# A two-directional gated scan inside an encoder layer: the base of eight tokens replaced by three more halving levels

## The chip, the core and the metric

The kernel runs on one core of a Trainium2 chip. The core has five engines that run side by side and wait for each other through semaphores: PE (TensorE, matmuls; its weight loads are shown as PEld), DVE (VectorE, elementwise work), ACT (ScalarE, activations and copies), POOL (GpSimd) and SP (SyncE, which issues most transfers). The metric is the device time of one execution in microseconds; lower is better. A profile is one execution with every instruction's start and duration.

## What is computed

One encoder layer for 1024 tokens of width 1024. The normed input is projected into the columns of two token mixers: a convolution module, and a two-directional recurrence (HGRN2) of 8 heads with 128 channels. The recurrence is what the change touches:

```python
def _chunk_gated_scan(q, k, v, lf):
    """S_t = diag(f_t) S_{t-1} + k_t v_t^T,  o_t = S_t^T q_t"""
...
def _bi_hgrn2(q, v, z_fwd, z_bwd, lb_fwd, lb_bwd):
    lf_f, k_f = _forget_log_and_key(z_fwd, lb_fwd)
    lf_b, k_b = _forget_log_and_key(z_bwd, lb_bwd)
    o_fwd = _chunk_gated_scan(qh, heads(k_f), vh, heads(lf_f))
    flip = lambda t: jnp.flip(t, axis=1)
    o_bwd = flip(_chunk_gated_scan(flip(qh), flip(heads(k_b)), flip(vh), flip(heads(lf_b))))
    return o_fwd + o_bwd
```

The weight between a query at token t and a key at token s is a sum over channels of q, k and the product of all forget gates f between s and t. After the mixers come output projections, a gated feed-forward part and a last norm. The large projections make up most of the matmuls; each float32 product is made of three products of split operands (high x high, high x low, low x high: lines 147 to 149).

## The kernel before

**Stages.** First norm and first projections; the paired projections with the convolution beside them; the scan stage (about 490 to 905 us in the profile), in which the rest of the projections (`dense`) is threaded between the scan's own steps; output projections; the feed-forward part; the last projection.

**The order of work.** PE runs in the order in which the program is written. The other engines' order is chosen by a scheduler when the kernel is built, from what each instruction depends on. The scan's loop runs over 8 heads and 2 halves of 512 tokens each: 16 half heads. After each piece of scan work it calls `between`, which first issues `FILL` = 1.3 pieces of `dense` (a piece is 6 matmuls of 128x512), then `BASE_STEPS` steps of the next half head's base (`ahead`), then one step of the previous head's outputs (`pending`). A half head has seven such pieces: four levels, two transposes and one product for the states.

**The scan of one half head.** The weights between tokens are built by halving: at level h, blocks of 2h tokens are split in two, and one product gives the weights between the two halves of every block, for both directions at once, since a pair (s, t) belongs to the forward direction on one side of the diagonal and to the backward direction on the other. For that, qF holds each query times the product of the gates from its block's middle, kG each key likewise, and tb the product over each whole block. After a level, kG and qF of half of the tokens are multiplied by tb of the neighbouring block, and tb itself is doubled. All channels lie on the 128 partitions, tokens along the free dimension.

- `scan_inputs` (L1072): loads q and the gate inputs z, and makes the keys `kk` and the gates f (ACT), then clamps f on DVE (L1093).
- `scan_base` (L1096): makes, for blocks of 8 tokens, products of gates within the block from its middle in tile DE and their reciprocals (L1117), from these Qh and Kh (scaled so that Qh times Kh is right for any pair within 8 tokens), then qF, kG and tb for blocks of 8. All of it is on DVE. `tt` (L1061) is the helper that issues every DVE multiplication, `keys` (L1064) that of the keys.
- `scan_levels` (L1156): `inside` (L1193) multiplies Kh by Qh for each 32 tokens, in both directions, into a bank "sc"; `level` (L1181) does levels 8 and 16 with a copy `A_t` of the keys on ACT (L1179), level 8 into the same bank, level 16 into bank "ob"; `blocks` (L1207) does levels 32 and 64. Each level is followed by the multiplications of kG, qF and tb. Masked copies on DVE (L1245 to L1249) gather the weights of each 32 tokens in D_t; the diagonal goes by tile dg and an addition (L1250). ACT puts all into S_t (L1252, L1254).
- `scan_states` (L1257): transposes kG (L1264) and multiplies it with v (L1273); `scan_outputs` (L1296) makes the outputs in bank "ob" (L1314).

**Banks.** PSUM has eight banks: three "mm" for `dense`, two "sc", two "tr", one "ob". Taking a bank again waits until its last reader has finished.

Of the kernel before, what the change touches and what calls it, by code (L numbers as in the profile page):

```python
# [29 lines left out]
BASE_STEPS = 2  # L30
# [16 lines left out]
def tile_hybrid_encoder(  # L47
# [868 lines left out]
    m_f, m_b, m_d, m_16 = [cp.tile([P, 32], U8, name=n) for n in ("m_f", "m_b", "m_d", "m_16")]  # L916

    def build_masks():
        it = mp.tile([P, 32], I32, tag="tm", name=nm("it"), bufs=4)
        ip = mp.tile([P, 32], I32, tag="tm", name=nm("ip"), bufs=4)  # L920
        G.iota(it, pattern=[[1, 32]], base=0, channel_multiplier=0)
        for g in range(0, P, 32):
            G.iota(ip[g : g + 32, :], pattern=[[0, 32]], base=0, channel_multiplier=1)
        xo = mp.tile([P, 32], I32, tag="tm", name=nm("xo"), bufs=4)
        V.tensor_tensor(xo, it, ip, op=ALU.bitwise_xor)
        fs = mp.tile([P, 4, 32], F32, tag="tm", name=nm("fs"), bufs=4)
        V.tensor_copy(fs[:, 0, :], xo)
        V.tensor_tensor(fs[:, 1, :], it, ip, op=ALU.subtract)
        ge = fs[:, 1, :]
        V.tensor_scalar(m_d, fs[:, 0, :], 0.0, None, op0=ALU.is_equal)  # L930
        V.tensor_scalar(m_16, fs[:, 0, :], 16.0, None, op0=ALU.is_ge)
        V.tensor_scalar(fs[:, 2, :], fs[:, 0, :], 8.0, None, op0=ALU.is_lt)
        V.tensor_scalar(fs[:, 3, :], ge, 0.0, None, op0=ALU.is_ge)
        V.tensor_tensor(m_f, fs[:, 2, :], fs[:, 3, :], op=ALU.mult)
        V.tensor_scalar(fs[:, 3, :], ge, 0.0, None, op0=ALU.is_lt)
        V.tensor_tensor(m_b, fs[:, 2, :], fs[:, 3, :], op=ALU.mult)
# [111 lines left out]
    NB = H // 8  # L1048
    DE = hp.tile([P, 2, 2, H], F32, name="DE")
    dg = hp.tile([P, 4, 32], F32, name="dg")  # L1050
    none = hp.tile([P, H], mybir.dt.bfloat16, name="none")
    E0, D0 = 0, 2 * H
    for o in (E0 + 3, D0 + 3):
        G.memset(view(DE, o, [[8, 2 * NB]]), 1.0)
    G.memset(none, 0.0)
    G.memset(dg, 0.0)

    N2 = 2 * NB

    def tt(o, a, b, op=ALU.mult):  # L1060
        V.tensor_tensor(o, a, b, op=op)  # L1061

    def keys(o, a, scale, b):
        V.scalar_tensor_tensor(o, a, scale, b, op0=ALU.mult, op1=ALU.mult)  # L1064
# [7 lines left out]
    def scan_inputs(i):  # L1072
# [5 lines left out]
        kk = hp.tile([P, 2, H], F32, tag="k", name=nm("k"), bufs=2)  # L1078
        nc.sync.dma_start(q, d_q[h][half])
        for d in range(2):  # L1080
            z = page(hp, "zi", 3)
            nc.sync.dma_start(z, d_z[d][h][half])
            A.activation(kk[:, d, :], z, AF.Sigmoid, scale=-1.0)
            A.activation(z, z, AF.Sigmoid)
            fo = view(f, d * H + 7 * d, [[8, NB], [1 - 2 * d, 8]])
            A.activation(
                fo,
                z.rearrange("p (b e) -> p b e", e=8),
                AF.Identity,
                scale=oml_of(d, h),  # L1090
                bias=lb_of(d, h),
            )
        V.tensor_scalar(f, f, MIN_FORGET, 1.0, op0=ALU.max, op1=ALU.min)  # L1093
        return q, f, kk, kscale[:, h : h + NH + 1 : NH]

    def scan_base(ins):  # L1096


        q, f, kk, ks = ins

        def two(t, *r):
            if len(r) == 1:
                return view(t, r[0], [[8, N2]])
            return view(t, r[0], [[r[1] - r[0], 2], [8, N2]])

        fv = lambda *r: two(f, *r)
        ed = lambda *r: two(DE, *r)
        D = D0


        V.tensor_copy(ed(2, D + 4), fv(3, 4))
        tt(ed(1, D + 5), fv(2, 4), fv(3, 5))
        yield
        tt(ed(0, D + 6), fv(1, 6), ed(1, D + 5))
        tt(ed(D + 7), ed(D + 6), fv(7))
        yield
        V.reciprocal(ed(D, 7), ed(0, D + 7))  # L1117
        yield

        fm = hp.tile([P, 2, NB], F32, tag="fm", name=nm("fm"), bufs=2)  # L1120
        turned = view(fm, NB, [[-NB, 2], [1, NB]])
        tt(turned, view(f, 0, [[H, 2], [8, NB]]), view(DE, E0, [[H, 2], [8, NB]]))
        tb = hp.tile([P, 3, NB], F32, tag="tb", name=nm("tb"), bufs=3)
        tt(tb[:, 0:2, :], turned, view(DE, D + 7, [[H, 2], [8, NB]]))
        V.tensor_copy(tb[:, 2, :], tb[:, 0, :])
        tt(ed(D + 1, 6), ed(D, 7), fv(1, 7))
        yield
        tt(ed(D + 2, 5), ed(D + 1, 6), fv(2, 6))
        tt(ed(4), ed(5), fv(5))
        yield  # L1130

        qF = hp.tile([P, 2, H], F32, tag="qF", name=nm("qF"), bufs=3)
        kG = hp.tile([P, 2, H], F32, tag="kG", name=nm("kG"), bufs=2)
        Qh = hp.tile([P, 2, H], F32, tag="Qh", name=nm("Qh"), bufs=1)
        Kh = hp.tile([P, 2, H], F32, tag="Kh", name=nm("Kh"), bufs=1)
        along = [[8, NB], [1, 8]]
        for d in range(2):
            m0, st = ((0, 1), (7, -1))[d]
            whole = [[8, NB], [st, 8]]
            tt(view(Qh, (1 - d) * H + m0, whole), view(q, m0, whole), view(DE, D + d * H, along))  # L1140
            yield
            keys(
                view(Kh, d * H + m0, whole),
                view(kk, d * H + m0, whole),
                ks[:, d : d + 1],
                view(DE, d * H, along),
            )
            yield
        both = [[H, 2], [8, NB], [1, 8]]
        tt(view(qF, 0, both), view(Qh, 0, both), view(fm, 0, [[NB, 2], [1, NB], [0, 8]]))  # L1150
        yield
        tt(view(kG, 0, both), view(Kh, 0, both), view(DE, D + 7, [[H, 2], [8, NB], [0, 8]]))
        yield
        yield qF, kG, [(Qh[:, 1 - d, :], Kh[:, d, :]) for d in range(2)], tb

    def scan_levels(base, S_t, Tt):  # L1156


        qF, kG, qk, tb = base

        def pairs(t, h):
            return view(t, 0, [[2 * h, H // (2 * h)], [H + h, 2], [1, h]])


        def near(t):
            return t.rearrange("p (c t) -> p c t", c=4)

        def slot(b, n):
            return b[:, n * P : (n + 1) * P]

        def each():
            for c in range(4):
                for g in range(0, P, 32):
                    yield c * P + g, slice(g, g + 32), slice(32 * c, 32 * c + 32)

        def level(b, h):

            A_t = page(hp, "A", 2)
            A.copy(A_t.rearrange("p (b x e) -> p b x e", x=2, e=h), pairs(kG, h))  # L1179
            for at, g, o in each():  # L1180
                T.matmul(  # L1181
                    b[g, o].rearrange("p (b x e) -> p b x e", x=2, e=h),
                    A_t[:, at : at + 32],
                    view(qF, at, [[2 * h, 16 // h], [H + h, 2], [1, h]]),
                    start=True,
                    stop=True,
                )

        def inside(b):

            for d in range(2):
                for at, g, o in each():
                    T.matmul(  # L1193
                        slot(b, 1 + d)[g, o],
                        qk[d][1][:, at : at + 32],
                        qk[d][0][:, at : at + 32],
                        start=True,
                        stop=True,
                    )
# [15 lines left out]
        def over(m):  # L1215
            return view(m, 0, [[0, 4], [1, 32]])

        D_t = hp.tile([P, 4, 32], F32, tag="D", name=nm("D"), bufs=2)
        b = bank("sc")
        inside(b)  # L1220
        for h in (8, 16, 32, 64):
            n, nb = H // (2 * h), H // h
            if h < 32:
                if h == 16:
                    b = bank("ob")
                level(b, h)
# [5 lines left out]
            tt(pairs(kG, h), pairs(kG, h), view(tb, 1, [[2, n], [nb - 1, 2], [0, h]]))  # L1232
            tt(pairs(qF, h), pairs(qF, h), view(tb, nb + 1, [[2, n], [nb - 1, 2], [0, h]]))
            if h < 64:
                tn = hp.tile([P, 3, NB], F32, tag="tb", name=nm("tb"), bufs=3)
                k = 3
                to = view(tn, 0, [[n, 3], [1, n]])
            else:
                k = 2
                to = view(Tt, 0, [[4, 2], [1, n]])  # L1240
            tt(to, view(tb, 0, [[nb, k], [2, n]]), view(tb, 1, [[nb, k], [2, n]]))
            tb = tn
            if h == 8:
                A.copy(D_t, near(slot(b, 0)))
                V.copy_predicated(D_t, over(m_f), near(slot(b, 1)))  # L1245
                for o, m in ((D_t, m_b), (dg, m_d)):
                    V.copy_predicated(o, over(m), near(slot(b, 2)))
            elif h == 16:
                V.copy_predicated(D_t, over(m_16), near(slot(b, 0)))  # L1249
                V.tensor_tensor(D_t, D_t, dg, op=ALU.add)  # L1250
# [135 lines left out]
    dense.fill(21)  # L1386
    pending = Stream(iter(()))
    for h in range(NH):
# [4 lines left out]
        for half in range(2):  # L1393
# [21 lines left out]
            qF, kG = base[0], base[1]  # L1415
# [403 lines left out]
```

## Time and profile before

| | |
|---|---|
| median of 3 runs | 1782.89 us (1781.95 to 1783.09) |
| profiled execution | 1784.03 us, of which 1782.3 us from its first to its last instruction (the span) |
| PE / DVE / ACT busy in the span | 1730.3 / 1257.5 / 773.8 us |
| mean granted TensorE clock | 0.993 |

How to read the lines in the next parts. A line of the waits is: who (engine, tile, line) waited for whom, total us, how many times, the longest. A line of the time line is: start in us, duration, engine, line, operation, output <- inputs, shape, number of merged instructions, and in brackets idle time before it and what ended it. A line of a group is: line, engine, operation, output <- inputs, shape, count, then busy us and mean ns of one, then the engine's idle time before these instructions. A line of a stretch is: from:to, length, then busy us and count of each engine in the order of its header. Matmuls overlap: dense ones start 0.23 us apart though each is shown with 0.39 us. A float32 matmul leaves two records.

### The profile page before, as it was taken

What the parts mean: (1) busy time and instruction counts of PE and PEld (TensorE: products, weight loads), DVE (VectorE), ACT (ScalarE), POOL (GpSimd) and SP (SyncE); (2) the same over time, 40 slices, a digit from 0 to 9 for tenths busy, and PEclk for the clock granted to TensorE, in tenths of its full rate; (3) what the DMA queues carried; (4) which work ended last, traced back from release to release, by engine and by line L of the source; (5) the groups of instructions that cost most, each with busy time, mean ns of one, the idle gap of its engine ahead of it and who ended that gap; (6) DMA issues with size and microseconds to landing.
All of it is one profiled execution on the core that took longest, in us unless ns stands there. A gap on an engine that the chain in (4) does not pass through costs nothing.

```text
span 1782.3 us, 27603 instructions
## 1 busy us (share of the span) xinstructions
PE 1730.3 (97%) x10614; PEld 1415.1 (79%) x10614; DVE 1257.5 (71%) x1892; ACT 773.8 (43%) x1486; POOL 153.7 (9%) x168
## 2 busy tenths in 40 slices
PE   8999999999999999999999999999999999999997
PEld 6878787888877777778878888778888888888885
DVE  5599999747679999999545567667667667444455
ACT  7343433334455656565551344344344344422123
POOL 2201111000000000000000002011111111000000
PEclk9999999999999999999999999999999999999998
DMA  8657787746663333435367665567767666534233
GB/s 286 216 154 179 189 185 183 197 152 207 195 190 109 117 119 120 131 102 189 126 209 223 189 207 182 149 147 149 153 150 155 144 150 136 159 103 127 76 91 136
DMA packets 321258, 284.29 MB, mean 160 GB/s; under 512 B 14942, under 2 KB 242022, under 8 KB 321126
## 3 DMA queue, kind: packets, MB, share of 16 engines
q1 hardware_dynamic: 279958, 250.01, 44.4%
q0 software_dynamic: 41168, 32.51, 12.8%
q8 instruction: 83, 1.36, 0.3%
q14 instruction: 49, 0.40, 0.1%
HBM read 189.40 MB, written 76.81 MB: 149 GB/s over the span
## 4 chain that ended last, share of the span: by engine, by line
PE 65%; DVE 16%; DMA 7%; issue 6%; ACT 4%; POOL 1%; SPq 0%; POOLq 0%; DVEq 0%; ACTq 0%
PE mm L147 16%; PE mm L148 16%; PE mm L149 16%; PE sc L147 3%; PE sc L149 3%; PE sc L148 3%; DVE acc L956 3%; DMA sw<-in_w_in_dram 3%; DVE kG L1061 2%; DVE wp L123 2%; DVE qF L1061 2%; DVE DE L1061 1%; PE tr L149 1%; PE tr L147 1%; PE tr L148 1%
## 5 line engine op out<-in xcount | busy, mean ns | idle before, releaser
L147 PE MATMUL mm<-hx,wp 128*128 128x512 f32 x1144 | 462.5, 404 | 9.9 <-DVE ev L718 4.7
L149 PE MATMUL mm<-hx,wp 128*128 128x512 f32 x1144 | 449.5, 393 | 1.4 <-DVE wp L123 1.4
L148 PE MATMUL mm<-hx,wp 128*128 128x512 f32 x1144 | 448.9, 392 | 0.0
L123 ACT CAST wp<-wr 128x1024 fp32r<-128x1024 f32 (+2 forms) x171 | 162.1, 949 | 352.9 <-PE mm L148 227.4
L147 PEld LDWEIGHTS mm<-hx,wp 128*128 128x128 f32 x1144 | 216.6, 189 | 57.0 <-DVE ev L718 7.6
L149 PEld LDWEIGHTS mm<-hx,wp 128*128 128x128 f32 x1144 | 216.3, 189 | 49.5 <-DVE wp L123 2.5
L123 DVE TENSOR_TENSOR wp<-wr,wp 128x1024 fp32r<-128x1024 f32 (+2 forms) x169 | 185.8, 1100 | 92.0 <-ACT wp L123 80.1
L148 PEld LDWEIGHTS mm<-hx,wp 128*128 128x128 f32 x1144 | 216.7, 189 | 41.1 <-issue 0.2
L956 DVE SCALAR_TENSOR_TENSOR acc<-gl,v_b,acc 128x1024 f32<-128x1024 f32 x120 | 149.0, 1277 | 0.5
L1670 DVE TENSOR_TENSOR xr<-mm,xr 128x512 f32<-128x512 f32 x48 | 33.2, 691 | 72.9 <-PE mm L149 72.9
L367 ACT COPY su<-mm 128x512 f32<-128x512 f32 x82 | 47.4, 578 | 56.2 <-PE mm L149 55.2
L123 ACT CAST wq<-sw 128x1024 fp32r<-128x1024 f32 x41 | 43.1, 1050 | 63.8 <-PE mm L148 29.8
L1519 DVE SCALAR_TENSOR_TENSOR tm<-gp,v_a,tm 128x512 f32<-128x512 f32 x88 | 65.9, 749 | 2.0
L147 PE MATMUL mm<-hy,wp 128*128 128x512 f32 x164 | 64.7, 395 | 2.0 <-ACT su L367 2.0
L147 PE MATMUL sc<-hy,wq 128*128 128x512 f32 x164 | 64.6, 394 | 0.0
L148 PE MATMUL mm<-hy,wp 128*128 128x512 f32 x164 | 64.3, 392 | 0.0
L149 PE MATMUL sc<-hy,wq 128*128 128x512 f32 x164 | 64.2, 391 | 0.0
L147 PE MATMUL tr<-hx,wp 128*128 128x512 f32 x164 | 63.9, 390 | 0.0
L149 PE MATMUL tr<-hx,wp 128*128 128x512 f32 x164 | 63.8, 389 | 0.0
L148 PE MATMUL tr<-hx,wp 128*128 128x512 f32 x164 | 63.8, 389 | 0.0
L148 PE MATMUL sc<-hy,wq 128*128 128x512 f32 x164 | 63.8, 389 | 0.0
L149 PE MATMUL mm<-hy,wp 128*128 128x512 f32 x164 | 63.7, 389 | 0.0
(362 smaller groups left out, 3413.8 us busy)
## 6 DMA issues: line engine op xcount, KB each, us to landing
wr<-in_w_in_dram SPq DMA_DIRECT2D x56, 512.0 KB, 4.3
wr<-in_ffn_w_up_dram SPq DMA_DIRECT2D x24, 512.0 KB, 6.1
sw<-in_ffn_w_up_dram SPq DMA_DIRECT2D x44, 256.0 KB, 3.3
d_g<-ft SPq DMA_DIRECT2D x44, 256.0 KB, 3.3
sw<-in_ffn_w_up_dram POOLq DMA_DIRECT2D x20, 512.0 KB, 8.6
sw<-in_w_in_dram SPq DMA_DIRECT2D x38, 256.0 KB, 3.2
d_z<-ev SPq DMA_DIRECT2D x32, 256.0 KB, 3.8
zi<-d_z SPq DMA_DIRECT2D x32, 256.0 KB, 2.6
```

Of the source, the lines that this page charges most:

```text
L123: parts = A.copy(hi, src), eng.tensor_tensor(lo, src, hi.bitcast(F32), op=ALU.subtract)
L147: T.matmul(acc, whi[:, k, :], ahi, start=first, stop=False, skip_group_check=again)
L148: T.matmul(acc, whi[:, k, :], alo, start=False, stop=False, skip_group_check=again)
L149: T.matmul(acc, wlo[:, k, :], ahi, start=False, stop=last, skip_group_check=again)
L367: A.copy(t, acc)
L956: V.scalar_tensor_tensor(acc, g[:, k : k + S], tap(k), acc, op0=ALU.mult, op1=ALU.add)
L1061: V.tensor_tensor(o, a, b, op=op)
L1519: V.scalar_tensor_tensor(c, g[:, o + k : o + k + H], vec("fdw", k * NF + j), c, op0=ALU.mult, op1=ALU.add,)
L1670: V.tensor_tensor(xr[i][half], acc, xr[i][half], op=ALU.add)
```

## The change

The base for blocks of 8 tokens goes, with DE, its reciprocals, Qh, Kh, fm and dg. In its place the same halving starts at blocks of one token:

- kG is made from the keys by one scaling per direction; qF is q times the gates of the other direction; tb is f itself.
- `scan_base` of the next half head now has five steps: scaling, key copy and qF; the diagonal's products (q with kG of both directions, accumulated) and level 1; level 2; level 4; the copies into D_t. Its PE products go into the four quarters of one "sc" bank. So PE work, which the base didn't have, is now issued in `between`, ahead of `pending`.
- `BASE_STEPS` becomes 1. The first half head's base is issued step by step within the opening fill, which stays at 21 pieces.
- `scan_levels` starts at level 8, whose bank is now "ob", as level 16's was and is. The key copy for a level is issued right after the multiplication of kG before it.
- The views `pairs` run over one half of the tile and then the other, where they alternated before. tb has two parts in place of three.
- Tiles: qF has 4 buffers (3 before), kG 3 (2; it takes the place of `kk`), A_t 3 (2), D_t 3 (2).

```diff
-BASE_STEPS = 2
+BASE_STEPS = 1
...
         f = hp.tile([P, 2, H], F32, tag="f", name=nm("f"), bufs=2)
-        kk = hp.tile([P, 2, H], F32, tag="k", name=nm("k"), bufs=2)
+        kG = hp.tile([P, 2, H], F32, tag="kG", name=nm("kG"), bufs=3)
...
+    def pairs(t, h, other=H):
+
+        return view(t, 0, [[other + h, 2], [2 * h, H // (2 * h)], [1, h]])
+
+    def key_blocks(kG, h):
+        A_t = page(hp, "A", 3)
+        A.copy(pairs(A_t, h, 0), pairs(kG, h))
+        return A_t
...
+    def level(b, A_t, qF, h):
+
+        for at, g, o in each():
+            T.matmul(
+                b[g, o].rearrange("p (b x e) -> p b x e", x=2, e=h),
+                A_t[:, at : at + 32],
+                view(qF, at, [[2 * h, 16 // h], [H + h, 2], [1, h]]),
+                start=True,
+                stop=True,
             )
...
+    def double(kG, qF, tb, h, to=None):
+
+        n, nb = H // (2 * h), H // h
+        tt(pairs(kG, h), pairs(kG, h), view(tb, 1, [[nb - 1, 2], [2, n], [0, h]]))
+        tt(pairs(qF, h), pairs(qF, h), view(tb, nb + 1, [[-(nb + 1), 2], [2, n], [0, h]]))
+        if to is None:
+            tn = hp.tile([P, 2, n], F32, tag=f"tb{h}", name=nm("tb"), bufs=2)
+            to = view(tn, 0, [[n, 2], [1, n]])
+        else:
+            tn = None
+        tt(to, view(tb, 0, [[nb, 2], [2, n]]), view(tb, 1, [[nb, 2], [2, n]]))
+        return tn
 
     def scan_base(ins):
...
+        q, f, kG, ks = ins
+        qF = hp.tile([P, 2, H], F32, tag="qF", name=nm("qF"), bufs=4)
+        D_t = hp.tile([P, 4, 32], F32, tag="D", name=nm("D"), bufs=3)
+        for d in range(2):
+            V.tensor_scalar(kG[:, d, :], kG[:, d, :], ks[:, d : d + 1], None, op0=ALU.mult)
+        A_t = key_blocks(kG, 1)
+        tt(qF, view(q, 0, [[0, 2], [1, H]]), view(f, H, [[-H, 2], [1, H]]))
         yield
...
+        b = bank("sc")
+        for at, g, o in each():
+            for d in range(2):
+                T.matmul(
+                    slot(b, 3)[g, o],
+                    kG[:, d, at : at + 32],
+                    q[:, at : at + 32],
+                    start=d == 0,
+                    stop=d == 1,
+                )
+        tb = f
+        for n, h in enumerate((1, 2, 4)):
+            level(slot(b, n), A_t, qF, h)
+            tb = double(kG, qF, tb, h)
+            A_t = key_blocks(kG, 2 * h)
             yield
...
+        A.copy(D_t, near(slot(b, 2)))
+        for n, m in ((0, m_1), (1, m_2), (3, m_d)):
+            V.copy_predicated(D_t, over(m), near(slot(b, n)))
+        yield qF, kG, A_t, tb, D_t
...
         for h in (8, 16, 32, 64):
-            n, nb = H // (2 * h), H // h
             if h < 32:
-                if h == 16:
-                    b = bank("ob")
-                level(b, h)
+                b = bank("ob")
+                level(slot(b, 0), A_t, qF, h)
...
             if h == 8:
-                A.copy(D_t, near(slot(b, 0)))
-                V.copy_predicated(D_t, over(m_f), near(slot(b, 1)))
-                for o, m in ((D_t, m_b), (dg, m_d)):
-                    V.copy_predicated(o, over(m), near(slot(b, 2)))
+                A_t = key_blocks(kG, 16)
+                V.copy_predicated(D_t, over(m_8), near(slot(b, 0)))
             elif h == 16:
                 V.copy_predicated(D_t, over(m_16), near(slot(b, 0)))
-                V.tensor_tensor(D_t, D_t, dg, op=ALU.add)
...
-    dense.fill(21)
+    dense.fill(6)
+    for _ in range(5):
+        cur.step(1)
+        dense.fill(3)
```

Level 1, 2 and 4 and the diagonal are 16, 16, 16 and 32 matmuls of 128x32 per half head; `inside`, which goes, was 32.

More of the change, by code (lines that the diff above doesn't have):

```diff
@@ L912, in oml_of @@
         return lbw[:, 3, d * NH + h : d * NH + h + 1]
-    m_f, m_b, m_d, m_16 = [cp.tile([P, 32], U8, name=n) for n in ("m_f", "m_b", "m_d", "m_16")]
+    m_d, m_1, m_2, m_8, m_16 = [
+        cp.tile([P, 32], U8, name=n) for n in ("m_d", "m_1", "m_2", "m_8", "m_16")
+    ]
     def build_masks():
@@ L1156, in scan_levels @@
-    def scan_levels(base, S_t, Tt):
[L1159 to L1199, printed above, removed]
```

116 lines of the change are left out of this document (23 added, 93 removed).

## The prediction

> **What bounds the kernel now.** I read the page's busy times first, then the scan's stretch alone, then who waits for whom in it, and last its time line engine by engine.
>
> ```profile
> span 1782.3 us, 27603 instructions
> ...
> PE 1730.3 (97%) x10614; PEld 1415.1 (79%) x10614; DVE 1257.5 (71%) x1892; ACT 773.8 (43%) x1486; POOL 153.7 (9%) x168
> ```
>
> TensorE (PE) is busy for 97% of the span, so over the whole program it sets the time. VectorE (DVE) at 71% is an average over stages, and the change lies in one stage. The scan runs from the first product of half head 0 (522.3 us) to that of half head 15 (867.6 us), which is 15 half heads of 23.0 us each:
>
> ```profile
> core 0: us, PE busy (x) PEld busy (x) DVE busy (x) ACT busy (x) POOL busy (x), PEclk, DMA share, GB/s
> 522.30:867.60 345.30, 329.25 (x4311) 269.18 (x4313) 314.19 (x647) 203.32 (x505) 13.74 (x14) 1.00 0.38 123
> ```
>
> Here VectorE is busy for 314.19 of 345.30 us (91%), ScalarE (ACT) for 59%, PE for 329.25 (95%) at a full granted clock. PE is idle for 345.30 - 329.25 = 16.05 us. Its waits in this stretch:
>
> ```profile
> PE ob L1181 <- DVE qF L1061: 5.7, 8, 0.9
> PE tr L1264 <- DVE kG L1061: 4.7, 6, 1.8
> PE sc L1207 <- DVE qF L1061: 3.2, 5, 1.2
> PE ob L1314 <- DVE D L1249: 1.1, 1, 1.1
> PE sc L1273 <- ACT kT L1266: 1.0, 2, 0.6
> ```
>
> Of the 16 us, 13.6 are waits for the multiplications of qF and kG between two levels: level 16 (L1181 into bank ob), blocks 64 (L1207), the transposes (L1264). The time line shows why those are late:
>
> ```profile
> 643.42 0.40 PE L149 MATMUL mm<-hx,wp 128*128 128x512 f32 x1
> 645.06 0.69 PE L1207 MATMUL sc<-qF,kG 128*64 128x64 f32 x16 [1.25 <-DVE qF L1061]
> ```
> ```profile
> 642.44 0.76 DVE L1064 SCALAR_TENSOR_TENSOR Kh<-k,kscale,DE 128x512 f32<-128x512 f32 x1
> 643.11 0.69 DVE L1061 TENSOR_TENSOR Qh<-q,DE 128x512 f32<-128x512 f32 x1
> 643.71 0.69 DVE L1061 TENSOR_TENSOR kG<-kG,tb 128x512 f32<-128x512 f32 x1
> 644.31 0.69 DVE L1061 TENSOR_TENSOR qF<-qF,tb 128x512 f32<-128x512 f32 x1
> ```
>
> Two products of the next half head's base (Kh, Qh) stand in VectorE's queue ahead of the kG and qF for which PE is waiting. So the stage is bounded by PE's own work, with 16 us on top in which a nearly full VectorE answers late. That is the most the change can win back, with some 4 us of refilling: between 643.42 and 645.06 lie 1.64 us where dense work takes 0.23, a loss of 1.41 where the row names 1.25, and 0.16 at each of the 22 waits makes 3.5.
>
> **The change, part by part. PE.** The base's own products (L1193, 32 matmuls of 128x32) go; 32 products for the diagonal and 16 for each of levels 1, 2 and 4 come. So each half head has 48 matmuls more, and none of its other PE work goes. What such blocks take:
>
> ```profile
> 634.83 0.73 PE L1193 MATMUL sc<-Qh,Kh 128*32 128x32 f32 x62
> ...
> 635.41 0.45 PE L1181 MATMUL sc<-qF,A 128*32 128x32 f32 x30
> 635.79 0.50 PE L147 MATMUL mm<-hx,wp 128*128 128x512 f32 x1
> 636.12 0.40 PE L148 MATMUL mm<-hx,wp 128*128 128x512 f32 x1
> ...
> 637.05 0.39 PE L149 MATMUL mm<-hx,wp 128*128 128x512 f32 x1
> 637.28 0.60 PE L1340 MATMUL tr<-ident,tm 128*128 128x128 f32 x4
> 637.81 0.46 PE L1181 MATMUL ob<-qF,A 128*32 128x32 f32 x32
> 638.20 0.50 PE L147 MATMUL mm<-hx,wp 128*128 128x512 f32 x1
> ```
>
> A matmul leaves two records. Level 16 alone occupies PE from 637.81 to 638.20, 0.39 us; the base's 64 records go in 635.41 - 634.83 = 0.58 us, 9.1 ns each, so a level right behind others of its kind takes 32 x 9.1 ns = 0.29. Level 1 follows the diagonal (0.29); levels 2 and 4 stand alone (0.39 each): 1.07 us per half head, 17 us for 16. A block after dense work costs about 0.08 more (the first matmul after a block is followed 0.33 us later, 635.79 to 636.12, where dense ones follow 0.23 apart, 637.05 to 637.28; entering costs nearly as much). Three blocks get a new entry, and each stands next to a block that had a way out anyway: 3 x 0.08 x 16 = 4 us. Bounds of both together: 96 records at 9.1 ns, 0.87 us, 14 us in all; three levels at 0.39 with full entry and exit of 0.2 each, 1.77 us, 28 us. I take 21.
>
> The diagonal's 32 matmuls replace 32 of the same size, but in another order: two accumulating matmuls in a row on the same 32 output rows, where each matmul now goes to the next 32. No row shows that. If the order is free it costs 0; if only one of the four row groups works at a time, 64 records take up to 4 x 0.58 us, +1.74 us or 28 us in all. The two records of one matmul are on one group today, and they don't slow the block, so I take a value near the low end, 3 us.
>
> Level 1 reads qF with single elements from alternating halves of the tile. VectorE's rows show what jumping costs there:
>
> ```profile
> L1061 DVE TENSOR_TENSOR DE<-DE,f 128x256 f32<-128x256 f32 x30 | 19.9, 662 | 0.1
> L1111 DVE COPY DE<-f 128x256 f32<-128x256 f32 x14 | 5.8, 418 | 0.0
> L1061 DVE TENSOR_TENSOR kG<-kG,tb 128x512 f32<-128x512 f32 x62 | 42.4, 685 | 0.4 <-ACT A L1179 0.3
> L1061 DVE TENSOR_TENSOR tb<-tb 128x96 f32<-128x96 f32 x15 | 3.8, 254 | 0.0
> L1061 DVE TENSOR_TENSOR tb<-tb 128x24 f32<-128x24 f32 x15 | 2.8, 184 | 0.0
> ```
>
> With two inputs at a step of eight elements, 256 elements cost 662 ns, as much as 512 with runs of eight or more (685); with one such input, 418. [...]
>
> **VectorE.** What goes is nearly everything that touches the tile DE, and the product of qF with it. The first row is the busy time of all VectorE instructions on DE in the same stretch:
>
> ```profile
> 522.30:867.60 345.30, 150.01 (x220) 0.00 (x0) 1.00 0.38 123
> ```
> ```profile
> L1061 DVE TENSOR_TENSOR qF<-Qh,fm 128x1024 f32<-128x1024 f32 x15 | 18.3, 1220 | 0.0
> L1250 DVE TENSOR_TENSOR D<-D,dg 128x128 f32<-128x128 f32 x15 | 4.3, 289 | 0.0
> L1245 DVE COPY_PREDICATED D<-m_f,sc 128x128 f32<-128x128 uint8 x15 | 4.4, 295 | 0.0
> L995 DVE TENSOR_SCALAR cx<-cx,v_a 128x512 f32<-128x512 f32 x8 | 4.2, 539 | 0.0
> ```
>
> Removed: (150.0 + 18.3 + 4.3) / 15 = 11.5 us per half head. Added: qF of 1024 elements 1.22; two scalings of kG at 0.54; three doublings, each with kG and qF of 512 (0.69 each, 4.11 in all; their steps are at most two elements, and from the tb rows 72 more elements at that step cost 70 ns, one ns each, so no penalty); three tb of 512, 256 and 128 elements, 0.69, 0.42 and 0.29; one masked copy more, 0.30. Sum 8.1. So VectorE loses 3.4 us per half head, 51 us in the stretch: 263 of 345 us, 76%. None of this is on the path by itself. It counts only through PE's 16 us.
>
> **ScalarE** gets three key copies more (A<-kG, 617 ns each):
>
> ```profile
> L1179 ACT COPY A<-kG 128x512 f32<-128x512 f32 x31 | 19.1, 617 | 21.3 <-DVE kG L1061 21.2
> ```
>
> That is 1.85 us per half head, 203 + 28 = 231 of 345 us, 67%, hidden beside PE. Such a copy waits for kG, now 21.2 us in all, and behind it in ScalarE's queue stand the evictions of dense work; three mm banks cover about two half tiles of it. I cost this at nothing; if the cover went, it would be of the size of a PE wait, 0.7 us each.
>
> **The new waits.** Levels 8 and 16 now share the one ob bank: level 16 must wait for the masked copy of level 8, one tb (0.20) and one copy (0.30) behind the qF for which it waits today. Cover is one fill of dense work, 635.79 to 637.28, 1.5 us, against qF, tb and copy of 0.69 + 0.20 + 0.30 = 1.2 us if VectorE is free at once. Without the cover it is 0.5 us x 16 = 8 us; I take 4. Levels 2 and 4 each wait for a qF product and a key copy behind the level before; between them lie a fill of 1.4 us or more and blocks 32 or 64 (0.4 to 0.6 us), against about 1.3 us of kG, qF and queue. Hidden, by some 0.5 us: bounds 0 and the 5.7 us that level 16's wait costs now, for each of three such places. PE is in order: behind each wait stands all dense work. Of the old 16 us I let 13 go, since the Kh and Qh that stood in the queue, the reciprocal and the two 1.2 us products leave the middle of the chain. Waits after: 3 + 4 = 7, so -9.
>
> No DMA is added, removed or reordered by its text; the inputs of a half head are asked for at the same place. The first base moves into the opening fill of 21 pieces, which stays 21 pieces.
>
> **Sum.** +21 (levels) + 3 (diagonal) + 1 (level 1's reads) - 9 (waits) = **+16 us**. The profiled execution took 1784.03 us (span 1782.3 and 1.7 around it), 1.1 above the median 1782.89; the sum is a difference inside the span and goes onto the median: **1798.9 us**.
>
> **Rivals.**
>
> 1. *All waits vanish and the blocks pack* (the other side: faster). Place: levels 16, blocks 64, transposes. The new records cost 14 us, the diagonal and level 1 nothing, the 16.05 us go entirely with 4 us of refill: 14 - 20 = -6, 1777 us. It decides from the point where each answer of VectorE comes within one dense fill, 1.5 us. For it: 51 us less in a queue that is 91% full. Against: level 16's chain gets longer.
> 2. *The relief just pays the price*: 21 - 20 = +1, 1784 us.
> 3. *Round trips.* PE waits at levels 2, 4 and the ob bank as it does at level 16 now (5.7 us per place), and the old waits stay: 21 + 3 + 1 + 17 = +42, 1825 us. For it: VectorE's work is now tied to PE level by level, where much of the base was free to run ahead. Against: 76% load.
> 4. *The diagonal runs one row group at a time*: +16 + 25 = +41, 1824 us. For it: no row shows this order; against: the two records of a matmul.
>
> That the change leaves its purpose undone (no VectorE time saved) would need the doublings at twice their rows' time; the tb rows speak against it, and it would end like rival 3.
>
> **How the numbers follow.** Forecast 0.47 (own range 1787 to 1811), rival 1 0.16, rival 2 0.14, rival 3 0.13, rival 4 0.10. A measurement of this kernel tells about 0.2%, 3.6 us, from no change: below 1779.3 is faster, above 1786.5 slower. Faster: rival 1 and a tail of 2, 0.18. Same: 0.13. Slower: 0.69. The range reaches down to most of rival 1 and up to rivals 3 and 4: 1778 to 1825.
>
> **What would show it.** VectorE's busy time in the scan near 76% of a stretch some 16 us longer; PE's count up by 16 x 96 = 1536 records; blocks of 32 records at 0.3 to 0.4 us, and one of 64 at 0.58 (rival 4: up to 2.3); a level 1 block as long as level 2's; PE's idle time in the scan near 7 us, mostly at bank ob. I am wrong if PE's idle time stays at 16 or grows, if it falls to nothing, or if the blocks cost other than their rows.

## The result and the profile after

| | before | after |
|---|---|---|
| median (4 runs each, side by side) | 1782.42 us | 1806.72 us |
| lowest to highest | 1780.56 to 1783.09 us | 1803.96 to 1808.28 us |
| ratio, 95% interval | | 1.0136 (1.0119 to 1.0154) |
| profiled execution / span | 1784.03 / 1782.3 us | 1807.26 / 1805.5 us |

The change costs 24.3 us, where the forecast was 16. Two lines of the page of after, busy time by engine and one DMA queue:

```profile
PE 1757.3 (97%) x12150; PEld 1433.9 (79%) x12150; DVE 1213.0 (67%) x1813; ACT 804.1 (45%) x1534; POOL 152.2 (8%) x165
...
q8 instruction: 95, 1.56, 0.3%
```

TensorE (PE) has 12150 - 10614 = 1536 records more, as counted beforehand, and is busy for 27 us longer; VectorE (DVE) is 44.5 us less busy. So the work moved as intended, from an engine at 71% to one at 97%. Queue q8 brings instructions; its 95 packets (83 before) matter further down.

From here on "the scan" is the stretch from the first kG transposes of half head 0 to those of half head 15, 15 half heads in each kernel, so that like stands beside like. The stretch of before, then that of after with two shorter stretches inside it (columns as in the prediction: busy time of PE, PEld, DVE, ACT, POOL, then granted clock, which is the share of the full TensorE clock that PE was given, DMA share, GB/s):

```profile
534.40:878.10 343.70, 328.90 (x4256) 269.09 (x4255) 309.77 (x638) 202.14 (x503) 13.74 (x14) 1.00 0.39 126
```
```profile
538.80:903.50 364.70, 353.73 (x5550) 286.23 (x5537) 265.66 (x552) 228.40 (x545) 12.83 (x14) 0.99 0.37 119
585.60:611.80 26.20, 23.25 (x370) 18.51 (x364) 16.97 (x31) 15.89 (x38) 1.84 (x2) 0.93 0.39 123
783.40:809.10 25.70, 22.78 (x372) 17.88 (x363) 17.85 (x35) 14.62 (x32) 1.64 (x1) 0.93 0.34 114
```

The scan is 21.0 us longer. PE is busy for 24.8 us more in it and idle for 11.0 us in place of 14.8. The other 2.2 us of the profiled difference lie outside: the transposes start 4.4 us later (534.4, 538.8; PE is busy for 4.2 us more there, with 255 more records), and what follows the scan is 2.2 us shorter (904.2, 902.0). The two short stretches are half heads in which the granted clock was 0.93: each holds one spell of 3.41 us at half clock, so by an estimate of half their length the two cost 2 x 1.7 = 3.4 us of the 24.8. That leaves 21.4 us of work, 1.42 us per half head. The kernel before has no such spell in the scan, but it has them elsewhere: while PE works, half clock lasts 3.41, 6.83 and 6.83 us there and five times 3.41 us in the kernel after, 17.1 us in each, and the mean granted clock is 0.993 in both. So the spells are a part of the scan's 21.0 us, but not of the whole 23.2 us.

Who waits for whom: two of the three waits for qF and kG in the scan of before (the third, of the transposes, is 4.7 us as in the prediction's rows), then the scan of after:

```profile
PE ob L1181 <- DVE qF L1061: 5.1, 7, 0.9
...
PE sc L1207 <- DVE qF L1061: 2.5, 4, 1.2
```

```profile
PE ob L1103 <- DVE D L1187: 4.9, 7, 2.0
PE sc L1103 <- issue: 2.7, 2, 2.1
PE ob L1103 <- DVE Sf L1220: 2.1, 5, 0.9
PE sc L1212 <- ACT kT L1205: 0.9, 2, 0.7
```

None of the three old waits for qF and kG is left. In their place stand 7.0 us at bank ob and 2.7 us that no engine explains. Of the 7.0 us, level 16 waits 4.9 for the masked copy of level 8 (L1187), and level 8 waits 2.1 for the state's accumulation (L1220), which reads the bank too.

The blocks are read from the time line of PE. First the diagonal and level 1 of one half head up to the next instruction (some records between the two blocks, where both interleave, are left out), then level 2 up to the next:

```profile
701.33 0.76 PE L1138 MATMUL sc<-q,kG 128*32 128x32 f32 x58
...
701.99 0.54 PE L1103 MATMUL sc<-qF,A 128*32 128x32 f32 x28
702.46 0.39 PE L1182 MATMUL sc<-none 128*128 128x512 bf16 x1
...
705.15 0.46 PE L1103 MATMUL sc<-qF,A 128*32 128x32 f32 x32
705.54 0.69 PE L1167 MATMUL sc<-qF,kG 128*64 128x64 f32 x16
```

Level 2 takes 705.54 - 705.15 = 0.39 us, as level 16 did before. Diagonal and level 1 take 702.46 - 701.33 = 1.13 us; the same 96 records before (634.83 to 635.79 in the prediction's rows) took 0.96. The same 1.13 us stand in 13 of the 16 half heads; the other three hold a wait or the half clock. So the diagonal's order and level 1's single elements cost 0.17 us together, 2.7 us for 16 half heads, where the forecast had 3 + 1.

One of the waits at bank ob, both engines in order of time:

```profile
794.42 1.22 DVE L123 TENSOR_TENSOR wp<-wr,wp 128x1024 fp32r<-128x1024 f32 x1
...
795.56 0.75 DVE L1281 SCALAR_TENSOR_TENSOR ev<-tr,v_a,og 128x512 f32<-128x512 f32 x1
796.22 0.68 DVE L1052 TENSOR_TENSOR qF<-qF,tb 128x512 f32<-128x512 f32 x1
796.82 0.29 DVE L1187 COPY_PREDICATED D<-m,ob 128x128 f32<-128x128 uint8 x1
...
797.26 0.46 PE L1103 MATMUL ob<-qF,A 128*32 128x32 f32 x32 [2.05 <-DVE D L1187]
```

The masked copy of 0.29 us sits behind qF, and qF behind two operations that have nothing to do with this bank (wp, the split of a weight for dense work, and ev, an output): 2.05 us of idle PE.

### The profile page after: what moved, and what is told of

It reads as the page before. It is cut to its first block, busy times and chain, and to the rows that moved or that the text cites. A ratio compares the mean times of both kernels' runs of the same rounds, so it can differ in the third digit from the quotient of the medians.

```text
span 1805.5 us, 30702 instructions
## 1 busy us (share of the span) xinstructions
PE 1757.3 (97%) x12150; PEld 1433.9 (79%) x12150; DVE 1213.0 (67%) x1813; ACT 804.1 (45%) x1534; POOL 152.2 (8%) x165
## 4 chain that ended last, share of the span: by engine, by line
PE 72%; DVE 9%; DMA 7%; ACT 5%; issue 4%; POOL 1%; SPq 1%; POOLq 0%; ACTq 0%; DVEq 0%
PE mm L147 17%; PE mm L149 16%; PE mm L148 16%; PE sc L147 3%; PE sc L149 3%; PE sc L148 3%; DVE acc L956 2%; PE ob L1253 2%; DVE wp L123 2%; PE tr L147 2%; PE tr L149 2%; PE tr L148 2%; DMA ev<-d_ga 1%; PE sc L1103 1%; DMA wr<-in_w_in_dram 1%
## 5 line engine op out<-in xcount | busy, mean ns | idle before, releaser
L1083 ACT COPY A<-kG 128x512 f32<-128x512 f32 x80 | 51.1, 643 | 73.2 <-DVE kG L1052 70.4
L1052 DVE TENSOR_TENSOR kG<-kG,tb 128x512 f32<-128x512 f32 x96 | 66.2, 690 | 18.6 <-PE sc L1167 9.6
L1052 DVE TENSOR_TENSOR qF<-qF,tb 128x512 f32<-128x512 f32 x96 | 66.0, 688 | 13.9 <-PE sc L1103 9.9
L147 PE MATMUL mm<-hy,wp 128*128 128x512 f32 x164 | 64.6, 394 | 1.4 <-ACT su L367 1.4
L147 PE MATMUL sc<-hy,wq 128*128 128x512 f32 x164 | 64.7, 394 | 0.0
L148 PE MATMUL mm<-hy,wp 128*128 128x512 f32 x164 | 64.3, 392 | 0.0
L149 PE MATMUL sc<-hy,wq 128*128 128x512 f32 x164 | 64.2, 391 | 0.0
L147 PE MATMUL tr<-hx,wp 128*128 128x512 f32 x164 | 64.0, 390 | 0.0
L149 PE MATMUL tr<-hx,wp 128*128 128x512 f32 x164 | 63.9, 389 | 0.0
```

The source lines that it names most:

```text
L147: T.matmul(acc, whi[:, k, :], ahi, start=first, stop=False, skip_group_check=again)
L148: T.matmul(acc, whi[:, k, :], alo, start=False, stop=False, skip_group_check=again)
L149: T.matmul(acc, wlo[:, k, :], ahi, start=False, stop=last, skip_group_check=again)
L1083: A.copy(pairs(A_t, h, 0), pairs(kG, h))
```

## The experiments

Each ratio is to runs of the kernel before on the same chip. "Scan" and "idle PE" are taken over the same 15 half heads as above. Where an edit adds lines, the line numbers behind it are one to three higher in its rows.

**The new wait alone.** The kernel after, with a "tr" bank for level 8, so that level 16 no longer waits for its masked copy.

```diff
-                b = bank("ob")
+                b = bank("tr" if h == 8 else "ob")
```

> The changed kernel with level 8 in a bank 'tr', so that level 16 no longer waits for the masked copy of level 8. Theory 'work' (the 48 added matmuls of a half head set the time, the waits are a remainder): the 7.0 us of PE's waits at bank ob in the scan fall to about 3 (level 16 still needs the qF before it), the time falls by 3 to 5 us against the changed kernel, to about 1802 us; +1.1% against before. Rival 'round trips' (PE is paced by VectorE's answers between the levels): the wait moves to the next level and the time stays within 1 us of 1806.

1802.18 us, ratio 1.0105 (1.0088 to 1.0122), as 'work' said. The stretch, its longest wait and the one at ob:

```profile
538.80:895.80 357.00, 351.05 (x5567) 283.68 (x5566) 264.80 (x554) 227.69 (x543) 12.83 (x14) 1.00 0.38 122
```
```profile
PE tr L1279 <- DVE ev L1281: 2.6, 2, 1.6
...
PE ob L1103 <- DVE qF L1052: 0.2, 1, 0.2
```

The wait at ob falls from 7.0 to 0.2 us, the granted clock of the scan is 1.00 in place of 0.99, and the scan is 7.7 us shorter; the medians differ by 4.5. Of the 7 us, 3.2 come back as waits at the "tr" banks (2.6 and 0.6), which the kernel after did not have; idle PE falls from 11.0 to 6.0 us. So the bank is a part of the loss, but only a part: 20 us stay.

**PE's blocks in the changed kernel, twice.** Levels 1, 2 and 4 are issued twice each into the same place.

```diff
-            level(slot(b, n), A_t, qF, h)
+            for _ in range(2):
+                level(slot(b, n), A_t, qF, h)
```

> The changed kernel with the matmuls of levels 1, 2 and 4 issued twice into the same place (48 more matmuls a half head, 1536 more records, nothing for VectorE or ScalarE). 'Work': another 96 records at 9 to 17 ns a half head, 14 to 27 us: 1821 to 1834 us. 'Round trips': PE's extra 0.9 us a half head is spent where it waited anyway, less than 8 us: under 1815. If fetching PE's instructions is a cost of its own, the gaps inside a level that no engine explains (2.7 us in two places) grow to 5 us or more.

1828.48 us, ratio 1.0264 (1.0248 to 1.0279): 21.8 us on top of the change for 48 matmuls per half head. The scan is 380.5 us long, 15.8 more than after, and idle PE is 15.3 us, so none of the added matmuls hides in a wait. Waits that no engine explains have grown from 2.7 to 5.0 us:

```profile
PE ob L1103 <- DVE D L1188: 6.0, 7, 1.8
PE sc L1103 <- issue: 3.7, 3, 2.0
...
PE sc L1168 <- issue: 1.3, 2, 0.7
```

The size is as 'work' expected. In the profile the first transposes start 9.1 us later (547.9 in place of 538.8), but 5.5 us of that is idle PE between 300 and 490 us, ahead of all that was changed, and this execution took 1833.42 us, 4.9 above the median.

**PE's blocks without the change.** The kernel before, with 48 matmuls of 128x32 on the identity added to each half head but the last, in three groups of 16, each behind a fill of dense work. VectorE has nothing more to do.

```diff
             def between(fill, n=0):
                 dense.fill(fill)
+                if 1 <= n <= 3 and i + 1 < NI:
...
+                            T.matmul(
+                                extra[0][g : g + 32, n * P + 32 * c : n * P + 32 * c + 32],
+                                ident[:, g : g + 32],
+                                ident[:, 32 * c : 32 * c + 32],
```

> The kernel before with 16 matmuls of 128x32 of the identity matrix, whose result is not used, at the three places of a half head at which the change issues levels 1, 2 and 4: the PE part of the change alone, tied to no other engine, with VectorE's load as before. 'Work': +17 to +25 us for the 48 matmuls, less up to 5 us of old waits that they cover: +13 to +24 us, 1796 to 1807 us. 'Round trips': the matmuls alone cost little, since they fall into waits: less than +8 us, under 1791.

1797.58 us, ratio 1.0079 (1.0064 to 1.0095).

```profile
536.10:894.40 358.30, 348.49 (x5611) 282.52 (x5600) 311.60 (x636) 200.45 (x501) 14.91 (x14) 1.00 0.38 121
```
```profile
PE ob L1181 <- DVE qF L1061: 5.6, 6, 1.6
PE tr L1264 <- DVE kG L1061: 1.6, 3, 0.7
```

PE is busy for 348.49 - 328.90 = 19.6 us more, 1.31 us per half head, and idle for 9.8 in place of 14.8 us: the extra matmuls fill some of the time in which PE would have waited for VectorE. Where the levels were issued twice, with the old waits gone, idle PE grew by 4.3 us instead: added work on PE was dearer where there was no such waiting to fill.

**VectorE's relief alone.** The kernel before, with copies in the place of the reciprocal and of four products of the base.

```diff
-        tt(ed(1, D + 5), fv(2, 4), fv(3, 5))
+        V.tensor_copy(ed(1, D + 5), fv(2, 4))
...
-        V.reciprocal(ed(D, 7), ed(0, D + 7))
+        V.tensor_copy(ed(D, 7), ed(0, D + 7))
```

> The kernel before with the reciprocals and four of the base's products of 256 elements left out, plain copies in their place (the weights within 8 tokens are then not the reference's): VectorE has 2.4 us less a half head, 38 us in all, and PE's work is untouched: the relief of the change alone. 'Work': only PE's 13.6 us of waits can shrink: -3 to -9 us, 1774 to 1780 us. 'VectorE-bound': most of the 38 us shows: -15 us or more, under 1768 us.

1771.39 us, ratio 0.9926 (0.9911 to 0.9942), 13 us faster.

```profile
536.30:868.80 332.50, 327.62 (x4256) 269.23 (x4255) 281.12 (x637) 201.04 (x503) 12.83 (x14) 1.00 0.40 130
```
```profile
PE ob L1181 <- DVE qF L1061: 1.4, 4, 0.5
PE tr L1264 <- DVE kG L1061: 1.4, 5, 0.4
```

PE's work is the same; its idle time falls from 14.8 to 4.9 us, the scan by 11.2. The gain lies between the two expectations, 3 to 9 and 15 or more, so both are missed. It is as large as the 13 us of old waits that the prediction let go, though the relief is smaller than the change's (VectorE's busy time falls by 28.7 us, in the change by 44.1): here no new wait at bank ob eats into it.

**The relief undone.** The kernel after, with one more product of 512 elements on VectorE, which nobody reads, behind each of the levels 1 to 16.

```diff
     def double(kG, qF, tb, h, to=None):
...
+        if h < 32:
+            more = page(hp, "more", 1)
+            tt(more, qF[:, 0, :], qF[:, 1, :])
```

> The changed kernel with one more VectorE product of 512 elements (0.69 us, its result unused) after the qF product of levels 1, 2, 4, 8 and 16: 3.4 us a half head, which puts VectorE's load back to that of before. 'Work': VectorE's load counts only through PE's waits, which grow by 0.2 to 0.5 us a half head: 3 to 8 us, 1810 to 1815 us. 'Round trips': each answer is 0.6 us later at three or four places a half head, 1.8 us or more: 30 us, about 1836 us.

1811.0 us, ratio 1.016 (1.0146 to 1.0174). VectorE is back at 305 us of busy time in the scan, but the kernel loses only 4.3 us, within the 3 to 8 of 'work'; idle PE grows from 11.0 to 13.7 us, and the waits at bank ob from 7.0 to 6.1 + 3.6 = 9.7 us. In the changed kernel VectorE's load is a side matter.

**Dense work moved (before).** The same amount of dense work, with more of it ahead of the places where PE waited.

```diff
+FILLS = (2.0, 1.0, 1.6, 1.5, 1.0, 1.0, 1.0)
...
-                between(FILL)
+                between(FILLS[n])
```

> The kernel before with the same 9.1 pieces of dense work a half head, dealt out as 2.0, 1.0, 1.6, 1.5, 1.0, 1.0, 1.0 over its seven places in place of 1.3 each: more cover in front of level 16, blocks 64 and the transposes, where PE waits 13.6 us for VectorE. 'Work': those waits are a matter of cover and fall to 4 to 8 us: 1773 to 1778 us, faster than both kernels. 'VectorE-bound': VectorE is 91% busy in this stage, so the waits only move to other places: within 2 us of 1782.

1786.5 us (12 runs), ratio 1.0013 (1.0002 to 1.0023): no gain, so 'work' is missed and 'VectorE-bound' holds. Idle PE is 18.4 us, at other places:

```profile
PE ob L1315 <- DVE D L1250: 5.2, 5, 1.2
PE sc L1208 <- DVE qF L1062: 5.0, 6, 1.6
PE tr L1265 <- DVE kG L1062: 3.9, 6, 1.4
```

With a VectorE that is 90% busy, dense work put ahead of one wait is missing at the next.

**Blocks moved together (after).** The first experiment's kernel, with the base's step ahead of the dense fill and one step at the head of the half head, so that a block enters from other small blocks and not from dense work.

```diff
+            if ahead is not None:
+                ahead.step(1)
...
-                dense.fill(fill)
...
+                dense.fill(fill)
```

> The changed kernel with level 8 in 'tr', and with the step of the next half head's base ahead of the dense work in place of behind it (its first step at the head of the half head): diagonal and level 1 directly behind level 8, level 2 behind level 16, level 4 behind the transposes. 'Work': three entries from dense work into small matmuls go, 0.1 to 0.2 us each, 5 to 10 us for 16 half heads: 1793 to 1798 us. 'Round trips': level 2 and level 4 now have less PE work between them and the VectorE product that they need, so waits grow and the time rises above 1806 us.

1808.7 us, ratio 1.0134 (1.0117 to 1.0151): 'work' is missed, and the waits grow as 'round trips' said.

```profile
PE sc L1103 <- ACT A L1083: 4.8, 9, 1.1
PE sc L1103 <- issue: 4.3, 4, 2.4
PE ob L1103 <- issue: 2.1, 2, 1.5
```

PE's busy time falls from 351.05 in the first experiment to 349.19 us, but now a level waits for its key copy on ScalarE (ACT), which the fill had hidden, and the unexplained waits grow to 6.4 us. The dense work between two levels costs an entry and pays for it as cover.

**A relief that computes the same: the base's first operations on GpSimd (before).**

```diff
-        V.tensor_copy(ed(2, D + 4), fv(3, 4))
-        tt(ed(1, D + 5), fv(2, 4), fv(3, 5))
+        G.tensor_copy(ed(2, D + 4), fv(3, 4))
+        G.tensor_tensor(ed(1, D + 5), fv(2, 4), fv(3, 5), op=ALU.mult)
...
-        tt(ed(0, D + 6), fv(1, 6), ed(1, D + 5))
-        tt(ed(D + 7), ed(D + 6), fv(7))
+        G.tensor_tensor(ed(0, D + 6), fv(1, 6), ed(1, D + 5), op=ALU.mult)
+        G.tensor_tensor(ed(D + 7), ed(D + 6), fv(7), op=ALU.mult)
```

> The kernel before, with the first four operations of every base (one copy of 256 elements and three products) on GpSimd instead of VectorE. What is computed stays the same. It takes 0.42 + 0.70 + 0.69 + 0.41 = 2.2 us per half head from VectorE, nearly as much as the copies in place of the reciprocal and four products did (2.4 us, 13 us won), and leaves all numbers right. Theory (PE's idle time in the scan follows VectorE's load): if GpSimd works beside VectorE undisturbed, the same gain, -7 to -13 us, 1769 to 1778, and the waits of PE in the scan fall from 14.8 us to 5 to 8; GpSimd's own products take about twice VectorE's time (its 512 elements took 1385 ns), 5 us per half head, in a stretch where it was busy for 13.7 of 344 us. Rival (the two engines hinder each other, one of them standing while the other moves data): VectorE's other rows grow, the reciprocal of 1756 ns and the 687 ns of a product first, or GpSimd's four take over 10 us and the reciprocal behind them comes late; then 1781 to 1795 and the waits of PE grow.

1813.66 us, ratio 1.0181 (1.0165 to 1.0196): slower, as the rival said, and beyond its 1781 to 1795. The stretch, GpSimd's longest group, then VectorE's and PE's longest waits:

```profile
535.80:911.10 375.30, 340.05 (x4252) 278.49 (x4255) 299.42 (x582) 201.83 (x503) 94.41 (x70) 0.96 0.36 116
```

```profile
L1111 POOL COPY DE<-f 128x256 f32<-128x256 f32 x14 | 39.8, 2844 | 227.0 <-DVE Kh L1064 195.3 <-ACT jk L1319 16.4 <-ACT kT L1266 15.4
```
```profile
DVE DE L1117 <- POOL DE L1115: 25.6, 12, 3.2
```
```profile
PE ob L1181 <- DVE qF L1061: 20.0, 8, 3.3
PE tr L1264 <- DVE kG L1061: 10.3, 8, 3.0
```

A copy that took 418 ns on VectorE shows 2844 ns on GpSimd (spans there are rough); VectorE stands for 25.6 us before its reciprocal, everything behind that in its queue is late, and idle PE is 35.3 us. VectorE's load has fallen, and PE waits more than twice as long. Of the rival's signs, this lateness is the clear one: the four operations take 5.7 us per half head on GpSimd, near the theory's 5, the reciprocal is as long as before (1755 ns), and the qF products grow only from 687 to 734 ns. So it isn't shown that the engines hinder each other much. Idle PE is also not the whole loss: the granted clock was 0.96 in this scan (1.00 in that of before), and PE is busy for 11.2 us more with the same work.

**A small dose: only the first copy, on ScalarE (before).**

```diff
-        V.tensor_copy(ed(2, D + 4), fv(3, 4))
+        A.copy(ed(2, D + 4), fv(3, 4))
```

> The kernel before, with only the first copy of every base (256 elements, 418 ns) on ScalarE instead of VectorE. What is computed stays the same. A small dose of the same relief: 0.42 us per half head, 6.3 us in the scan. Theory (idle time of PE in proportion to VectorE's load, 13 us won for 2.4 us per half head): -2 us, 1780 to 1783. Rival (the order in VectorE's queue decides, not the load): the gain has nothing to do with the dose, below -5 or above 0.

1798.08 us, ratio 1.0092 (1.0075 to 1.0109), 16 us slower, so the rival holds: the gain doesn't go by the dose. PE's work is the same within 1.3 us, its idle time 27.8 us:

```profile
PE ob L1181 <- DVE qF L1061: 10.0, 9, 1.9
PE sc L1207 <- DVE qF L1061: 7.1, 8, 1.7
```

The longest of the first kind on the time line:

```profile
564.97 0.70 DVE L1061 TENSOR_TENSOR kG<-kG,tb 128x512 f32<-128x512 f32 x1
...
565.84 1.76 DVE L1117 RECIPROCAL DE<-DE 128x256 f32<-128x256 f32 x1
...
567.50 0.64 DVE L1061 TENSOR_TENSOR qF<-qF,tb 128x512 f32<-128x512 f32 x1
...
568.29 0.46 PE L1181 MATMUL ob<-qF,A 128*32 128x32 f32 x32 [1.89 <-DVE qF L1061]
```

The next base's reciprocal has come to stand between kG and the qF for which PE waits. Of the 60 such products of qF in the scan, 12 have a reciprocal between the last kG product ahead of them and themselves; in the kernel before 4 have. PE's order is the same in both; VectorE's was chosen anew by the scheduler when the copy left its queue.

**Two tests of that.** First the kernel before with the reciprocal in two halves, each a step of its own:

```diff
-        V.reciprocal(ed(D, 7), ed(0, D + 7))
+        V.reciprocal(ed(D), ed(0))
+        yield
+        V.reciprocal(ed(7), ed(D + 7))
```

> The kernel before, with the reciprocal of every base (256 elements, 1756 ns) issued as two of 128 elements in two steps. What is computed stays the same, and so does VectorE's load but for some 0.1 us more per half head. In the run with one copy on ScalarE the longest waits of PE (1.9, 1.6 and 1.4 us) had that reciprocal directly ahead of the qF that PE wanted. Theory A (the longest single instruction that can stand ahead of a qF sets PE's waits): the waits of PE in the scan fall from 14.8 us to 9 to 12 and the time by 2 to 6 us, 1776 to 1780. Theory B (the load sets them): no gain, 1781 to 1786. Theory C (each edit makes the scheduler order VectorE's queue anew, and the order it happens on decides): anything from 1772 to 1800, with PE's work the same within 1.5 us and only its waits changed.

Then the kernel before with three base steps ahead of each pending step:

```diff
-BASE_STEPS = 2
+BASE_STEPS = 3
```

> The kernel before, with three base steps in place of two ahead of each pending step, so that a base is issued in four pieces of the loop rather than six. Nothing is computed otherwise, no instruction is added or removed and none changes its engine: only the order in VectorE's queue changes. Theory C (the order decides): PE's busy time in the scan stays at 329 us within 1.5 us and its waits differ from 14.8 us by more than 4 us, either way. Theory B (the load sets the waits): waits of 12 to 18 us, 1780 to 1786.

1780.32 us, ratio 0.9990 (0.9981 to 1.0000), and 1780.1 us, ratio 0.9992 (0.9982 to 1.0002). Idle PE is 14.6 and 13.9 us, 14.8 before; a reciprocal stands in such a place six times (as a half, 0.96 us) and four times. Neither edit matters beyond 0.2%, so the waits are as theory B (the load) said, and neither the reciprocal's length nor a new order as such is worth much where few products have it ahead of them. For the copy on ScalarE the reciprocals are seen beside the waits, but no run moved them back, so that cause is likely and not shown.

## Why the prediction was right, and where it was off

- **Direction and main term: right.** PE's work was to grow by 21 + 3 + 1 = 25 us for 16 half heads, 23.4 for 15; in the scan it grew by 21.4 without the half-clock spells, in the whole execution by 27.0. The three added blocks alone, in the kernel before, cost 1.31 us of PE's time per half head. That this is just the forecast's 21 / 16 = 1.31 is chance: there all three stand behind dense work, which by the forecast's rows is 3 x (0.39 + 0.08) = 1.41.
- **Diagonal and level 1: right.** 2.7 us in place of 4. Rival 4 (one row group at a time) would by the forecast's estimate have made the pair of blocks up to 1.74 us longer; it is 0.17 longer. The diagonal's last record starts 701.99 - 701.33 = 0.66 us after its first, where the 64 records of before take 0.57. No run shows the 1 us for level 1's reads by itself: what is measured is the 0.17 us of both blocks together.
- **VectorE: right.** 265.66 us of busy time in the scan, forecast 263. The groups of the added operations have the forecast's prices, 1.22 us for qF and 0.49 for a scaling that was put at 0.54:

```profile
L1052 DVE TENSOR_TENSOR qF<-q,f 128x1024 f32<-128x1024 f32 x13 | 15.9, 1221 | 0.1
...
L1131 DVE TENSOR_SCALAR kG<-kG,kscale 128x512 f32<-128x512 f32 x26 | 12.7, 487 | 18.9 <-ACT kG L1071 17.2 <-PE mm L148 1.3
```

- **ScalarE: right.** 228.40 us, forecast 231, and no level of the changed kernel waits for its key copy. The run with the blocks moved together shows what that cover is worth: 4.8 us.
- **Waits: the step that was mis-sized.** The prediction put them at -9 (13 of 16 us gone, 4 new at bank ob). The old ones went more fully than said: of the 12.3 us for qF and kG in the scan of before nothing is left. But bank ob took 7.0 us, not 4: level 16's wait is 4.9, and the 2.1 of level 8 were not thought of. Nor were the 2.7 us of waits that no engine explains. So idle PE fell by 3.8 us in place of 9, in the scan (14.8 to 11.0) and in the whole execution (1782.3 - 1730.3 = 52.0 to 1805.5 - 1757.3 = 48.2). This is what lies between the forecast and the time: where the forecast had 25 - 9 = 16, the profiled executions have 27.0 - 3.8 = 23.2 us.
- **Rival 1 (faster) and rival 2 (even): refuted.** The relief can win what the forecast gave it (13 us from a part of it alone). But the scan of after would take 364.7 - 11.0 - 3.4 = 350.3 us with no idle PE and no half clock at all, and that of before took 343.7. The added work alone decides the sign.
- **Rival 3 (round trips): half right about the place, wrong about the size.** Bank ob is the one place that became a round trip; levels 2 and 4 did not.

No version that computes the same beat the kernel before by more than 0.1%. The best of the changed kernel is the one with level 8 in a "tr" bank, 1802.18 us.

## What to carry to other kernels

Here one engine was busy for 97% of the span. Work moved onto it cost nearly its full duration (27.0 us more busy time, a span 23.2 us longer), while work taken from another could win at most that engine's idle time, 14.8 us in the scan (4.9 were left with the relief alone): compare the two sums first. Small work added to the bound engine can hide in its waits only while there are such waits (5 us of 19.6 in the kernel before, none in the kernel after), and where two steps in a row shared a bank, the second waited for whatever stood in the reader's queue (7.0 us here, 0.2 with a bank of its own). What such a wait costs shows only when it is taken away, since a part of it can come back elsewhere (3.2 of the 7 us here). And an edit to an engine whose order a scheduler chooses is also an edit to that order: one copy of 418 ns moved away from VectorE cost 16 us, probably by the order, which no run changed alone.

## What was not expected of the hardware

**Instruction fetch.** The longest wait without a releaser lies in the middle of a block:

```profile
600.41 0.31 PE L1103 MATMUL sc<-qF,A 128*32 128x32 f32 x10
602.79 0.44 PE L1103 MATMUL sc<-qF,A 128*32 128x32 f32 x19 [2.08 <-issue]
```

On queue q8 a packet of 16 KB ran from 599.56 to 601.32, and PE went on 1.5 us after its end. The second such wait (0.63 us, to 801.71) ends 1.2 us after a packet in the same way (798.84 to 800.52). These two packets, of 1.75 and 1.68 us, are the longest of the 43 that begin in the scan of after, and PE's waits between 490 and 960 us name no other without a releaser. The kernel before has none, though one packet in its scan took 1.79 us (from 694.22). The number of packets grows with the number of matmuls: 83 before, 95 after with 1536 records more, so one more packet for every 128 records, or 256 instructions with their weight loads. By an estimate from that, dense matmuls, 0.23 us apart, use such a packet up in about 29 us; 128 records of small ones at 9.1 ns take 1.2 us, less than this packet's own 1.75 (the 95 packets take 0.88 to 1.75). That the fetch is the cause rests on these times and counts; no run changed the fetch alone.

**Half clock after one wait.** PE's first dense matmuls after that wait:

```profile
605.07 0.63 PE L148 MATMUL mm<-hx,wp 128*128 128x512 f32 x1
605.49 0.63 PE L149 MATMUL mm<-hx,wp 128*128 128x512 f32 x1
```

They start 0.42 us apart in place of 0.23. The granted clock was half from 604.1 for 3.41 us, and again from 798.6; in the 3.41 us ahead of each spell lies one wait of over 2 us (2.08 and 2.05). All spells of this execution start a whole number of 3.41 us apart (85, 57, 37, 76 and 180 times), so stretches of that length can be laid end to end from one of them, to see how the idle time falls into them. Two stretches, from the kernel after and from the one with the levels twice (length, busy time of PE and its records, granted clock, DMA share, GB/s):

```profile
600.70:604.10 3.40, 1.32 (x56) 1.00 1.00 313
```
```profile
611.30:614.70 3.40, 1.72 (x81) 1.00 0.64 183
```

The first, with 2.08 us of idle PE, is followed by half clock. In the second PE is idle for 3.40 - 1.72 = 1.68 us, and the granted clock is 1.00 from 538 to 620 us. In the scans of before and after, laid out in this way, the two stretches at full clock with the most idle PE (2.08 and 2.05 us, both in the kernel after) were each followed by the start of a spell, and none of the others, with 1.49 us or less. That is a count of two profiles; no run moved a wait within its stretch.
